# Layer norm in a two-block transformer: sums from a constant matrix as weights, mean, variance and root in all partitions, no broadcasts

## The chip, the cores and the metric

The kernel runs on one core of one Trainium2 chip. The metric is device time in microseconds of one execution, as the median of several runs. TensorE (PE) multiplies matrices, VectorE (DVE) and ScalarE (ACT) work elementwise, GpSimd (POOL) does elementwise work too, and SyncE (SP) issues most DMAs. Each engine takes its instructions from a queue of its own, in order, and waits on semaphores where it needs another engine's result.

## The reference

Two transformer blocks with two layers each run over 256 tokens of width 1024, the second with 16 tokens put in front (272). Between the matrix products stand ten layer norms of the residual stream. What the change touches is this:

```python
def layer_norm(x, g, b):
    xf = x.astype(jnp.float32)
    mu = jnp.mean(xf, -1, keepdims=True)
    var = jnp.mean(jnp.square(xf - mu), -1, keepdims=True)
    return ((xf - mu) * lax.rsqrt(var + EPS) * g + b).astype(x.dtype)
...
for i in range(DEPTH):
    ...
    x = layer_norm(DN_ALPHA * x + m, ln1_g[i], ln1_b[i])
    x = layer_norm(DN_ALPHA * x + conv_ffn(x, ffn_w_up[i], ffn_conv_w[i], ffn_conv_b[i], ffn_w_down[i]),
                   ln2_g[i], ln2_b[i])
    gate = jax.nn.sigmoid(x @ ple_w_gate[i] + ple_b_gate[i])
    x = x + gate * (p[i] @ ple_w_proj[i])
...
h = layer_norm_2(DEEPNORM_ALPHA * h + 0.5 * swiglu(h, ffn1_wg[l], ffn1_wu[l], ffn1_wd[l]),
               ln_gain[l, 0], ln_bias[l, 0])
...
h = layer_norm_2(DEEPNORM_ALPHA * h + mix, ln_gain[l, 1], ln_bias[l, 1])
h = layer_norm_2(DEEPNORM_ALPHA * h + 0.5 * swiglu(h, ffn2_wg[l], ffn2_wu[l], ffn2_wd[l]),
               ln_gain[l, 2], ln_bias[l, 2])
```

## The kernel before, in words

**Layout.** The residual X lies transposed in SBUF: 128 partitions, 8 chunks of the width, 256 or 272 tokens along the free axis. So a layer norm sums over partitions and chunks, and its mean and root differ from column to column. Each product of fp32 matrices is made of three matmuls of high and low halves (L405 to L407; L465, L466 and L468 are the same three in another order): XH and XL are the halves of X, wh and wl those of a weight chunk. The class Stream brings the weights in order: a DMA fills wraw, ScalarE makes wh (L315), VectorE wl (L317), some chunks ahead of their use.

**The norms.** Ten objects of the class LN follow one another, called LN1 to LN9 and the final norm here. LN1 to LN4 and LN8, LN9 have 256 tokens, LN5 to LN7 have 272 and so three token tiles instead of two. LN1 to LN4 stand ahead of the first block's up and gate projections and take the entry "early" of LN_AT. LN8 stands ahead of the query projection of the second block. While the product that makes X runs, evac (L566) adds each pair of chunks into X and gathers two partial sums, ln_d of X and ln_q of its squares, and raw_split makes XH and XL of the not yet normalised X.

**Hiding a norm.** The next product begins on that raw X: its first group runs over four output blocks and eight chunks kc. hook (L618) is called ahead of each kc and places the norm's steps there by the table LN_AT: stats, root and spread with the first finals. stats (L638) sums ln_d and ln_q over the partitions with one-column matmuls into a small tile [128 tokens, 2 to 4], and VectorE makes mean and variance of it. root takes the square root (ScalarE, L522) and one step of refinement (VectorE, L526 to L529, with a reciprocal). bcast (L535) turns a column of a small tile into a row in all partitions, by a transpose on TensorE: for the mean in root, for the root in spread. ScalarE copies both rows to SBUF (ln_m, ln_s). POOL waits for the root (L668) and subtracts the mean from X, two chunks at a time (L670). finals (L679) multiplies chunk by chunk with the root, which is read from PSUM (ln_w, L689), applies gain and bias (ScalarE L695 and L697, VectorE or POOL L699) and makes the new XL (L683). fix (L713) corrects the first group, which ran on raw X, in its output (L721).

**Order.** The program is written in the order of the calls, and each engine's queue follows it. W.fill(1) in hook issues a wh on ScalarE and the wl of the chunk before on VectorE at the kc's of LN_FILL. The final norm has no product to hide under: finish (L726) calls its steps one after the other, and the output's DMAs go out as chunks are done.

Of the kernel before, what the change touches and what calls it, by code (L numbers as in the profile page):

```python
# [10 lines left out]
F32 = mybir.dt.float32  # L11
F32R = mybir.dt.float32r
I32 = mybir.dt.int32
AF = mybir.ActivationFunctionType
ALU = mybir.AluOpType

P = 128
DM = 1024
# [6 lines left out]
EPS = 1e-5  # L25
# [2 lines left out]

AT = 96
XW, XO = 320, 12
HO = 4
XS = {"block1": 0, "block2": NMETA, "kv": 0}
# [113 lines left out]
TAIL = {"": 10, "gate0": 18, "gate1": 21, "aq": 24, "wo": 0, "cout": 14, "ao": 14}  # L148
LOOK = {"": 1, "aq": 2}

LN_AT = {"": (1, 2, 4), "early": (0, 1, 3)}
LN_FILL = {"": (0, 5), "aq": (0,), "f21": (0, 3)}

FILL = {"": (1, 2), "gate0": (0, 1), "gate1": (0, 1), "aq": (0, 1), "up1": (1, 1)}
# [69 lines left out]
def block_kernel(ctx: ExitStack, tc: tile.TileContext, wd, xin, pin, pos, vecs, con1, con2, wa2, fb, out):  # L224
# [3 lines left out]
    mm = nc.tensor.matmul  # L228
    V, A, G = nc.vector, nc.scalar, nc.gpsimd
# [133 lines left out]
    def cst(name, n, rows=P):  # L363
        return con[:rows, CON[name]:CON[name] + n]
# [25 lines left out]
    def aux():  # L390
        i = ps["n"][1] % 4
        if ps["mode"] == "aux":
            ps["n"][1] += 1
            if i >= 2:
                return ps["ext"].tile([P, 512], F32, tag="aux", name="aux")
        return ps["aux"].tile([P, 512], F32, tag="aux", name="aux")
# [111 lines left out]
    def token_tiles(T):  # L508
        return [0, P] + ([T - P] if T > 2 * P else [])
# [22 lines left out]
    def bcast(dst, r, T):  # L532

        for j, c0 in enumerate(token_tiles(T)):
            trp(dst[:, c0:c0 + P], r[:, j:j + 1].broadcast_to([P, P]), eye)  # L535
# [6 lines left out]
    class LN:  # L542
# [23 lines left out]
        def evac(self, m, n, psum):  # L566
            T = self.T
            xv = self.x(m, n)
            if m == 0:
                V.scalar_tensor_tensor(xv, xv, ALPHA, psum, op0=MUL, op1=ADD)  # L570
                self.s = self.buf("ln_s")[:, 0, :]
                V.tensor_tensor(self.s, self.x1(0), self.x1(1), op=ADD)
                if not self.final:
                    for k, nm in enumerate((self.g, self.b)):
                        c = VEC[nm] + self.j
                        split(self.XH[:, :, TT + k], self.XL[:, :, TT + k], vec[:, c:c + 8])
                return
            V.tensor_tensor(xv, psum, xv, op=ADD)  # L578
            sq = self.buf("ln_w", 2, 3)[:, :n, :]
            A.activation(sq, xv, AF.Square)  # L580
            if m <= 4:
                if m == 2:
                    self.D, self.Q = self.buf("ln_d", 2), self.buf("ln_q", 2)
                d, q = (self.x(0, 2), self.sq0) if m == 2 else (self.D, self.Q)
                V.tensor_tensor(self.D, d, xv, op=ADD)
                G.tensor_tensor(self.Q, q, sq, op=ADD)  # L586
                if m == 4:
                    D, Q = self.D, self.Q
                    self.D, self.Q = D[:, 0, :], Q[:, 0, :]
                    V.tensor_tensor(self.D, self.D, D[:, 1, :], op=ADD)  # L590
                    G.tensor_tensor(self.Q, self.Q, Q[:, 1, :], op=ADD)
            elif m == 6 or not self.final:
                V.tensor_tensor(self.D, self.D, xv[:, 0, :], op=ADD)
                V.tensor_tensor(self.Q, self.Q, sq[:, 0, :], op=ADD)
                self.parts = ((self.D, self.Q),)
            else:
                self.parts = ((self.D, self.Q), (xv[:, 0, :], sq[:, 0, :]))
            for i in range(m, m + n):
                self.raw_split(i)
# [18 lines left out]
        def hook(self, kc, name):  # L618

            h = LN_AT["early" if self.early else ""]  # L620
            if kc == h[0]:
                self.stats()
            if kc == h[1]:
                self.root()
            if kc == h[2]:
                self.spread()
                self.late = []
                self.finals(range(kc))
            elif kc > h[2]:
                self.finals((kc - 1,))  # L630
            if kc in LN_FILL.get(name, LN_FILL[""]):
                W.fill(1)
            if kc == 7:
                self.ndr = self.dls[:, 0, :]
                V.scalar_tensor_tensor(self.ndr, self.ndr, -1.0, self.R[:, :self.T], op0=MUL, op1=MUL)
                self.adds = []

        def stats(self):  # L638
            tt = token_tiles(self.T)
            n = len(tt)  # L640
            st = aux()
            order = [(i, w, j) for i in range(len(self.parts)) for w in range(2) for j in range(n)]
            for i, w, j in order:
                mm(st[:, 4 * w + j:4 * w + j + 1], self.parts[i][w][:, tt[j]:tt[j] + P], ones, start=(i, w, j) == order[0], stop=(i, w, j) == order[-1])  # L644
            self.dl = small.tile([P, 4], F32, tag="ln_dl", name="ln_dl")[:, :n]
            nd = small.tile([P, 4], F32, tag="ln_nd", name="ln_nd")[:, :n]
            self.v = small.tile([P, 4], F32, tag="ln_v", name="ln_v")[:, :n]
            V.tensor_scalar(self.dl, st[:, 0:n], 1.0 / DM, None, op0=MUL)
            V.scalar_tensor_tensor(nd, self.dl, -1.0, self.dl, op0=MUL, op1=MUL)
            V.scalar_tensor_tensor(self.v, st[:, 4:4 + n], 1.0 / DM, nd, op0=MUL, op1=ADD)  # L650

        def root(self):
            T = self.T
            DL = aux()
            bcast(DL, self.dl, T)
            self.dls = self.buf("ln_m")

            def between():
                A.activation(self.dls[:, 0, :], DL[:, :T], AF.Copy)

            self.r = rsqrt_eps(self.v, len(token_tiles(T)), between)
            if self.final:
                V.tensor_tensor(self.x(0, 2), self.x(0, 2), DL[:, None, :T].broadcast_to([P, 2, T]), op=SUB)
            if self.func:
                A.activation(dummy, epst, self.func)

            after = small.tile([P, 4], F32, tag="ln_nd", name="ln_nd")[:, :len(token_tiles(T))]
            G.tensor_copy(after, self.r)  # L668
            for m in range(2 if self.final else 0, 8, 2):
                G.tensor_tensor(self.x(m, 2), self.x(m, 2), self.dls.broadcast_to([P, 2, T]), op=SUB)  # L670

        def spread(self):
            self.R = aux()
            bcast(self.R, self.r, self.T)
            if not self.final:
                self.rs = self.buf("ln_s")
                A.activation(self.rs[:, 0, :], self.R[:, :self.T], AF.Copy)  # L677

        def finals(self, ms):  # L679
            T = self.T  # L680
# [4 lines left out]
            for m in ms:  # L685
                if m % 2 == 0:
                    self.t = self.buf("ln_w", 2, 3)
                t = self.t[:, m % 2, :]
                V.tensor_tensor(t, self.x1(m), self.R[:, :T], op=MUL)  # L689
                g, b = vc(self.g, self.j + m), vc(self.b, self.j + m)  # L690
                if self.final and m % 2:
                    A.activation(self.x1(m), t, AF.Identity, scale=g, bias=b)
# [33 lines left out]
        def finish(self):  # L726
            self.stats()
            self.root()
            self.spread()
            self.finals(range(8))  # L730


# [854 lines left out]
```

## Time and profile before

| | us |
|---|---|
| median of 3 runs (lowest, highest) | 1754.02 (1750.91, 1759.49) |
| the profiled execution | 1752.61 |
| its span on the core | 1750.8 |
| mean granted clock of TensorE | 0.986 of full speed |

The rows further down come from this one profiled execution. A matmul's record covers its passage through the array, so successive matmuls overlap: the pace is read from their starts, not from their durations. On the other engines too an instruction may begin shortly before its predecessor's end. A bracket at the end of a timeline row gives the idle time of that engine ahead of the instruction, and what ended it.

### The profile page before, as it was taken

The page shows a single profiled execution, that of the slowest core. Times are in us where ns is not written, and L with a number is a line of the kernel's source. Part 1 is how long each engine was busy: PE and PEld are TensorE (multiplying, and loading weights), DVE is VectorE, ACT ScalarE, POOL GpSimd, SP SyncE. Part 2 cuts the span into 40 slices and gives each one's busy share as a digit, 9 for nine tenths or more (in the row PEclk, how much of TensorE's full clock was granted, in tenths as well). Part 3 has the DMA queues.
Part 4 walks back from the last instruction along what each step waited for, and adds up shares of the span by engine and source line. Part 5 has one row for each costly group of instructions (what it writes and reads, how often), then busy time and mean ns, then how long its engine had stood idle before and what let it go on. Part 6 is the DMA issues. An engine that isn't in the chain of part 4 may idle for free. (4 is left out here: it accounts for less than half of the span.)

```text
span 1750.8 us, 34305 instructions
## 1 busy us (share of the span) xinstructions
PE 1710.1 (98%) x13954; PEld 1676.0 (96%) x13954; DVE 1212.7 (69%) x1951; ACT 997.3 (57%) x1575; POOL 217.8 (12%) x244
## 2 busy tenths in 40 slices
PE   7999999999999999999999999999999999999997
PEld 6999999997899999999999999999999999899997
DVE  6777898777579977755567787547665566787553
ACT  5666776566468765654445556445645553766542
POOL 6100211030012210200002030000200002020002
PEclk9999999999999999999999999999999999999998
DMA  6444466535445665365544627554446654237551
GB/s 224 133 140 161 134 217 211 199 122 201 146 144 161 219 208 185 122 230 178 181 157 135 226 98 240 171 180 170 154 162 196 196 181 162 71 135 253 193 181 37
DMA packets 82990, 298.18 MB, mean 170 GB/s; under 512 B 9319, under 2 KB 10487, under 8 KB 82832
## 3 DMA queue, kind: packets, MB, share of 16 engines
q1 hardware_dynamic: 82176, 294.13, 50.6%
q8 instruction: 109, 1.79, 0.4%
q0 software_dynamic: 656, 1.87, 0.4%
q14 instruction: 49, 0.40, 0.1%
HBM read 294.91 MB, written 1.05 MB: 169 GB/s over the span
## 5 line engine op out<-in xcount | busy, mean ns | idle before, releaser
L315 ACT ACTIVATE wh<-wraw 128x1024 fp32r<-128x1024 f32 (+1 forms) x557 | 578.8, 1055 | 352.8 <-PE acc L406 297.6
L405 PE MATMUL acc<-XH,wh 128*128 128x256 f32 (+3 forms) x2660 | 748.7, 281 | 2.8 <-ACT wh L315 1.7
L407 PE MATMUL acc<-XH,wl 128*128 128x256 f32 (+3 forms) x2660 | 745.5, 280 | 1.0 <-DVE wl L317 1.0
L406 PE MATMUL acc<-XL,wh 128*128 128x256 f32 (+3 forms) x2660 | 745.2, 280 | 0.0
L317 DVE TENSOR_TENSOR wl<-wraw,wh 128x1024 fp32r<-128x1024 f32 (+1 forms) x557 | 678.8, 1249 | 71.1 <-ACT wh L315 67.2
L405 PEld LDWEIGHTS acc<-XH,wh 128*128 128x128 f32 x2660 | 501.3, 188 | 3.7 <-ACT wh L315 1.9
L407 PEld LDWEIGHTS acc<-XH,wl 128*128 128x128 f32 x2660 | 500.7, 188 | 1.5 <-DVE wl L317 1.3
L406 PEld LDWEIGHTS acc<-XL,wh 128*128 128x128 f32 x2660 | 501.1, 188 | 0.0
L405 PE MATMUL acc<-hs,wh 128*128 128x256 f32 (+1 forms) x1044 | 291.8, 279 | 0.0
L406 PE MATMUL acc<-hs,wh 128*128 128x256 f32 (+1 forms) x1044 | 290.6, 278 | 0.0
L407 PE MATMUL acc<-hs,wl 128*128 128x256 f32 (+1 forms) x1044 | 290.6, 278 | 0.0
L406 PEld LDWEIGHTS acc<-hs,wh 128*128 128x128 f32 x1044 | 195.9, 188 | 0.2
L405 PEld LDWEIGHTS acc<-hs,wh 128*128 128x128 f32 x1044 | 195.9, 188 | 0.2
L407 PEld LDWEIGHTS acc<-hs,wl 128*128 128x128 f32 x1044 | 195.9, 188 | 0.0
L1312 DVE SCALAR_TENSOR_TENSOR sg<-acc,sg 128x272 f32<-128x272 f32 (+1 forms) x84 | 36.2, 432 | 185.5 <-ACT sg L1311 185.4
L586 POOL TENSOR_TENSOR ln_q<-ln_w 128x512 f32<-128x512 f32 (+1 forms) x10 | 14.2, 1422 | 978.2 <-ACT ln_w L580 978.2
L580 ACT ACTIVATE ln_w<-X 128x512 f32<-128x512 f32 (+3 forms) x40 | 21.3, 533 | 92.2 <-DVE X L578 92.1
L1120 POOL TENSOR_TENSOR gl<-cv,gl 128x256 f32<-128x256 f32 x44 | 39.2, 892 | 185.6 <-ACT gl L1119 102.1
L578 DVE TENSOR_TENSOR X<-acc,X 128x512 f32<-128x512 f32 (+3 forms) x40 | 22.4, 561 | 56.0 <-PE acc L407 56.0
L1311 ACT ACTIVATE sg<-acc 128x272 f32<-128x272 f32 (+1 forms) x84 | 32.5, 389 | 48.0 <-PE acc L407 47.5
L689 DVE TENSOR_TENSOR ln_w<-X,aux 128x256 f32<-128x256 f32 (+1 forms) x80 | 33.1, 417 | 37.3 <-ACT ln_s L677 29.3
L695 ACT ACTIVATE XH<-ln_w,vec 128x256 fp32r<-128x256 f32 (+1 forms) x72 | 42.3, 600 | 27.0 <-DVE ln_w L689 26.3
(418 smaller groups left out, 2311.8 us busy)
## 6 DMA issues: line engine op xcount, KB each, us to landing
wraw<-wd SPq DMA_DIRECT2D x555, 512.0 KB, 4.2
X<-xin SPq DMA_DIRECT2D x4, 272.0 KB, 6.1
out_t<-X SPq DMA_DIRECT2D x3, 256.0 KB, 2.7
wraw<-wd SPq DMA_DIRECT2D x2, 256.0 KB, 4.2
praw<-pin POOLq DMA_DIRECT2D x2, 256.0 KB, 2.9
fpt<-con POOLq DMA_DIRECT2D x2, 256.0 KB, 4.1
cum<-con POOLq DMA_DIRECT2D x1, 408.0 KB, 4.3
vec<-vecs SPq DMA_DIRECT2D x1, 283.0 KB, 7.0
```

The costliest lines, as they stand in the source:

```text
L315: A.activation(h[:, k], r[:, k], AF.Copy)
L317: self.low = lambda h=h, l=l, r=r, i=i: [V.tensor_tensor(l[:, k], r[:, k], f32(h[:, k]), op=SUB) for k in self.cuts(i)]
L405: mm(o, wh, xh, start=start, stop=False)
L406: mm(o, wh, xl, start=False, stop=False)
L407: mm(o, wl, xh, start=False, stop=stop)
L578: V.tensor_tensor(xv, psum, xv, op=ADD)
L580: A.activation(sq, xv, AF.Square)
L689: V.tensor_tensor(t, self.x1(m), self.R[:, :T], op=MUL)
L695: A.activation(self.XH[:, m, self.t0:TT], t, AF.Identity, scale=g, bias=b)
L1120: G.tensor_tensor(gl, t[:, 0, :], gl, op=MUL)
L1311: A.activation(s, psum[:, 0, :], AF.Silu)
L1312: V.scalar_tensor_tensor(s, psum[:, 1, :], 0.5, s, op0=MUL, op1=MUL)
```

## The change

The sums are made by two matmuls for each pair of partial sums, with a 128 x 128 matrix of 1/256 (the constant c256, which mid in L605 uses already) as weights: each partition then holds the sum of every token. Mean, variance and root are worked out there on all tokens, with tiles [128, 256] or [128, 272]. The broadcasts, spread, and the small tile ln_dl are gone. The subtraction of the mean from the first two chunks moves from POOL to VectorE. ln_w takes the root from the SBUF tile ln_s instead of PSUM. LN_AT calls root right behind stats. AT keeps later addresses where they were.

```diff
-AT = 96
+AT = 224
...
-LN_AT = {"": (1, 2, 4), "early": (0, 1, 3)}
+LN_AT = {"": (1, 1, 4), "early": (0, 0, 3)}
...
-                    self.D, self.Q = D[:, 0, :], Q[:, 0, :]
+                    self.D, self.Q, self.scratch = D[:, 0, :], Q[:, 0, :], Q
...
             if kc == h[2]:
-                self.spread()
                 self.late = []
                 self.finals(range(kc))
...
-                V.scalar_tensor_tensor(self.ndr, self.ndr, -1.0, self.R[:, :self.T], op0=MUL, op1=MUL)
+                V.scalar_tensor_tensor(self.ndr, self.ndr, -1.0, self.rs[:, 0, :], op0=MUL, op1=MUL)
...
         def stats(self):
-            tt = token_tiles(self.T)
-            n = len(tt)
-            st = aux()
-            order = [(i, w, j) for i in range(len(self.parts)) for w in range(2) for j in range(n)]
-            for i, w, j in order:
-                mm(st[:, 4 * w + j:4 * w + j + 1], self.parts[i][w][:, tt[j]:tt[j] + P], ones, start=(i, w, j) == order[0], stop=(i, w, j) == order[-1])
...
+            self.S = [aux()[:, :self.T] for _ in range(2)]
+            n = len(self.parts)
+            for w in range(2):
+                for i, p in enumerate(self.parts):
+                    mm(self.S[w], cst("c256", P), p[w], start=i == 0, stop=i == n - 1)
 
         def root(self):
             T = self.T
-            DL = aux()
-            bcast(DL, self.dl, T)
+            sd, sq = self.S
             self.dls = self.buf("ln_m")
...
-            self.r = rsqrt_eps(self.v, len(token_tiles(T)), between)
-            if self.final:
-                V.tensor_tensor(self.x(0, 2), self.x(0, 2), DL[:, None, :T].broadcast_to([P, 2, T]), op=SUB)
+            dl, v, t = self.dls[:, 0, :], self.scratch[:, 0, :], self.scratch[:, 1, :]
+            self.rs = self.buf("ln_s")
+            r = self.rs[:, 0, :]
+            A.activation(dl, sd, AF.Copy, scale=0.25)
+            V.scalar_tensor_tensor(v, dl, -1.0, dl, op0=MUL, op1=MUL)
+            V.scalar_tensor_tensor(v, sq, 0.25, v, op0=MUL, op1=ADD)
+            A.activation(r, v, AF.Sqrt, bias=epst)
+            V.tensor_scalar(v, v, EPS, None, op0=ADD)
+            V.tensor_tensor(self.x(0, 2), self.x(0, 2), self.dls.broadcast_to([P, 2, T]), op=SUB)
+            V.reciprocal(r, r)
+            V.tensor_tensor(t, r, r, op=MUL)
+            V.scalar_tensor_tensor(t, t, -0.5, v, op0=MUL, op1=MUL)
+            V.scalar_tensor_tensor(r, t, 1.5, r, op0=ADD, op1=MUL)
             if self.func:
                 A.activation(dummy, epst, self.func)
 
-            after = small.tile([P, 4], F32, tag="ln_nd", name="ln_nd")[:, :len(token_tiles(T))]
-            G.tensor_copy(after, self.r)
-            for m in range(2 if self.final else 0, 8, 2):
+            after = small.tile([P, 4], F32, tag="ln_nd", name="ln_nd")
+            G.tensor_copy(after, r[:, :4])
+            for m in (2, 4, 6):
                 G.tensor_tensor(self.x(m, 2), self.x(m, 2), self.dls.broadcast_to([P, 2, T]), op=SUB)
-
-        def spread(self):
-            self.R = aux()
-            bcast(self.R, self.r, self.T)
-            if not self.final:
-                self.rs = self.buf("ln_s")
-                A.activation(self.rs[:, 0, :], self.R[:, :self.T], AF.Copy)
...
-                V.tensor_tensor(t, self.x1(m), self.R[:, :T], op=MUL)
+                V.tensor_tensor(t, self.x1(m), self.rs[:, 0, :], op=MUL)
```

In what follows, names stand for tiles and "128x256" for partitions and elements. VectorE's queue at LN1 before, from the sums to the second multiplication with the root (aux is the PSUM tile with the sums, later that with the broadcast root):

```order
L648 TENSOR_SCALAR ln_dl<-aux 128x2
L649 SCALAR_TENSOR_TENSOR ln_nd<-ln_dl 128x2
L650 SCALAR_TENSOR_TENSOR ln_v<-aux,ln_nd 128x2
L317 TENSOR_TENSOR wl<-wraw,wh 128x1024
L523 TENSOR_SCALAR ln_v<-ln_v 128x2
L526 RECIPROCAL rs_r<-rs_r 128x2
L527 TENSOR_TENSOR rs_t<-rs_r 128x2
L528 SCALAR_TENSOR_TENSOR rs_t<-rs_t,ln_v 128x2
L529 SCALAR_TENSOR_TENSOR rs_r<-rs_t,rs_r 128x2
L689 TENSOR_TENSOR ln_w<-X,aux 128x256
L699 TENSOR_SCALAR X<-ln_w,vec 128x256
```

The same stretch of VectorE's queue after (with the line numbers of the changed file):

```order
L653 SCALAR_TENSOR_TENSOR ln_q<-ln_m 128x256
L654 SCALAR_TENSOR_TENSOR ln_q<-aux,ln_q 128x256
L656 TENSOR_SCALAR ln_q<-ln_q 128x256
L657 TENSOR_TENSOR X<-X,ln_m 128x2x256
L658 RECIPROCAL ln_s<-ln_s 128x256
L659 TENSOR_TENSOR ln_q<-ln_s 128x256
L660 SCALAR_TENSOR_TENSOR ln_q<-ln_q 128x256
L661 SCALAR_TENSOR_TENSOR ln_s<-ln_q,ln_s 128x256
L317 TENSOR_TENSOR wl<-wraw,wh 128x1024
L680 TENSOR_TENSOR ln_w<-X,ln_s 128x256
L690 TENSOR_SCALAR X<-ln_w,vec 128x256
```

The weight split wl stood between variance and root and now stands behind the root; a subtraction on X has come in, and ln_w reads ln_s.

ScalarE's queue at the same place, before:

```order
L315 ACTIVATE wh<-wraw 128x1024
L522 ACTIVATE rs_r<-ln_v,epst 128x2
L659 ACTIVATE ln_m<-aux 128x256
L665 ACT_TABLE_LOAD
L665 ACTIVATE dummy<-epst 128x1
L677 ACTIVATE ln_s<-aux 128x256
```

And after:

```order
L652 ACTIVATE ln_m<-aux 128x256
L655 ACTIVATE ln_s<-ln_q,epst 128x256
L663 ACT_TABLE_LOAD
L663 ACTIVATE dummy<-epst 128x1
L315 ACTIVATE wh<-wraw 128x1024
```

The wh of the weight stream stood ahead of the square root and now stands behind it and the table load; the copy of the broadcast root is gone.

## Rows read from the trace of the kernel before

**Rows 1.** the page's busy shares: engine, busy us (share) xinstructions.

```profile
PE 1710.1 (98%) x13954; PEld 1676.0 (96%) x13954; DVE 1212.7 (69%) x1951; ACT 997.3 (57%) x1575; POOL 217.8 (12%) x244
```

**Rows 2.** TensorE's waits: line <- releaser: us in total, times, longest.

```profile
PE aux L406 <- DVE XL L683: 3.8, 1, 3.8
...
PE acc L465 <- ACT sg L1139: 2.7, 1, 2.7
...
PE acc L412 <- DVE XL L506: 2.4, 1, 2.4
...
PE acc L405 <- DVE cv L1115: 0.9, 1, 0.9
...
PE acc L405 <- DVE ln_d L721: 0.2, 1, 0.2
```

**Rows 3.** timeline of TensorE, LN1: start, us, instruction [idle before <-releaser].

```profile
185.64 0.28 PE L407 MATMUL acc<-ph,wl 128*128 128x256 f32 x1
...
186.76 0.28 PE L466 MATMUL acc<-XH,wl 128*128 128x258 f32 x1
...
191.01 0.28 PE L407 MATMUL acc<-XH,wl 128*128 128x258 f32 x1
...
191.47 0.28 PE L406 MATMUL acc<-XL,wh 128*128 128x258 f32 x1
```

**Rows 4.** timeline of TensorE around one sum of L605.

```profile
155.27 0.28 PE L407 MATMUL acc<-O,wl 128*128 128x256 f32 x1
...
155.94 0.28 PE L406 MATMUL acc<-O,wh 128*128 128x256 f32 x1
```

**Rows 5.** timeline of VectorE, LN1; the last line is LN3.

```profile
187.20 1.22 DVE L317 TENSOR_TENSOR wl<-wraw,wh 128x1024 fp32r<-128x1024 f32 x1
...
188.99 0.17 DVE L529 SCALAR_TENSOR_TENSOR rs_r<-rs_t,rs_r 128x2 f32<-128x2 f32 x1
192.03 0.42 DVE L689 TENSOR_TENSOR ln_w<-X,aux 128x256 f32<-128x256 f32 x1 [2.87 <-ACT ln_s L677]
192.49 0.82 DVE L699 TENSOR_SCALAR X<-ln_w,vec 128x256 f32<-128x256 f32 x1
...
525.40 0.42 DVE L689 TENSOR_TENSOR ln_w<-X,aux 128x256 f32<-128x256 f32 x1 [4.74 <-ACT ln_s L677]
```

**Rows 6.** timeline of ScalarE and POOL, LN1.

```profile
191.54 0.38 ACT L677 ACTIVATE ln_s<-aux 128x256 f32<-128x256 f32 x1 [1.16 <-PE aux L535]
...
189.36 5.11 POOL L670 TENSOR_TENSOR X<-X,ln_m 128x512 f32<-128x512 f32 x4
```

**Rows 7.** VectorE by shape: xcount | busy us, mean ns | idle before, releasers.

```profile
L526 DVE RECIPROCAL rs_r<-rs_r 128x2 f32<-128x2 f32 x9 | 1.4, 158 | 0.0
...
L526 DVE RECIPROCAL rs_r<-rs_r 128x4 f32<-128x4 f32 x2 | 0.3, 171 | 0.0
...
L699 DVE TENSOR_SCALAR X<-ln_w,vec 128x256 f32<-128x256 f32 x13 | 12.4, 957 | 0.5
...
L689 DVE TENSOR_TENSOR ln_w<-X,aux 128x272 f32<-128x272 f32 x24 | 10.3, 430 | 12.0 <-ACT ln_s L677 12.0
```

**Rows 8.** all instructions of line 564: ns min/median/max, first and last start.

```profile
L564 DVE SCALAR_TENSOR_TENSOR XL<-X,vec,XH x72: 472/496/1608, 158.9 to 1553.9; 128x256 fp32r<-128x256 f32 x48, 128x272 fp32r<-128x272 f32 x24
```

**Rows 9.** timeline of VectorE, LN8; TensorE's window behind it: us, busy (x), PEclk, DMA.

```profile
1484.07 0.42 DVE L689 TENSOR_TENSOR ln_w<-X,aux 128x256 f32<-128x256 f32 x1 [7.15 <-POOL X L670]
1484.52 3.35 DVE L699 TENSOR_SCALAR X<-ln_w,vec 128x256 f32<-128x256 f32 x1
...
1489.30:1494.80 5.50, 5.43 (x25) 0.50 0.01 1
```

**Rows 10.** timeline of VectorE and POOL, final norm.

```profile
1741.09 0.16 DVE L529 SCALAR_TENSOR_TENSOR rs_r<-rs_t,rs_r 128x2 f32<-128x2 f32 x1
1741.17 0.68 DVE L663 TENSOR_TENSOR X<-X,aux 128x512 f32<-128x512 f32 x1
...
1741.45 3.86 POOL L670 TENSOR_TENSOR X<-X,ln_m 128x512 f32<-128x512 f32 x3
```

More of the change, by code (lines that the diff above doesn't have):

```diff
@@ L645, in stats @@
[L645 to L650, printed above, removed]
+            self.S = [aux()[:, :self.T] for _ in range(2)]
@@ L652, in root @@
+            n = len(self.parts)
+            for w in range(2):
+                for i, p in enumerate(self.parts):
+                    mm(self.S[w], cst("c256", P), p[w], start=i == 0, stop=i == n - 1)
         def root(self):
             T = self.T
-            DL = aux()
-            bcast(DL, self.dl, T)
+            sd, sq = self.S
             self.dls = self.buf("ln_m")
-            def between():
-                A.activation(self.dls[:, 0, :], DL[:, :T], AF.Copy)
-            self.r = rsqrt_eps(self.v, len(token_tiles(T)), between)
@@ L728, in finish @@
             self.root()
-            self.spread()
             self.finals(range(8))
```

## The prediction, made before the changed kernel ran

> **What bounds the kernel now.** I read the page's busy shares first. TensorE is busy for 1710.1 of 1750.8 us [rows 1], so the time falls only by what is taken off TensorE's queue, and it rises wherever TensorE is made to wait. Next I read the view of TensorE's waits [rows 2], which tells at which layer norms TensorE already waits for the VectorE work behind them: 3.8 us for XL of L683 (the norm ahead of the query projection, LN8), 2.7 us for sg, where ScalarE itself waits for the new X (LN4), 2.4 us for XL of L506 (LN2), 0.9 us for cv (LN1) and 0.2 us for the corrected group of L721 (LN7). At such a norm a VectorE that comes later by d makes TensorE later by d, and a TensorE that comes earlier only waits longer. Last I read the timelines around one norm [rows 3 to 6], which give the price of each step.
>
> **What TensorE saves.** Before, four one-column matmuls lie between the start of the L407 matmul at 185.64 and the L466 at 186.76: 1.12 us for what is otherwise two steps of TensorE's pace, 0.115 us here (the mean of [rows 1], 1710.1 us over 13954 matmuls, is 0.12), so 0.89 us for the sums [rows 3]. The broadcast of the root lies between 191.01 and 191.47: 0.46 us for two steps of 0.115, so 0.23 us, and there are two broadcasts. A 256-token norm now costs 0.89 + 0.46 = 1.35 us of TensorE. The new sums are two matmuls of the shape that L605 already runs; one of those lies between 155.27 and 155.94 and costs 0.67 - 0.23 = 0.44 us [rows 4], so two cost 0.88 us. The saving is 0.47 us a norm, for six norms (a tenth, the final one, has nothing beside it). The three 272-token norms have a third token tile, so half as many sums and broadcasts again: 2.02 us against 0.94, a saving of 1.08. Together 6 x 0.47 + 3 x 1.08 = 6.1 us, if TensorE has no one to wait for.
>
> **What VectorE pays.** Before, its chain from sum to root works on 2 to 4 columns, under 0.2 us a step: it gives way to a weight split of 1.22 us and ends at 188.99 + 0.17 = 189.16. Then VectorE idles 2.87 us until the root has been broadcast and copied, and L689 starts at 192.03 [rows 5]. After, the same steps are 256 columns wide. From the rows: a two-input step of this width starts the next 0.45 us on (0.42 at 192.03), a ScalarE pass 0.38 us [rows 6], a 512-wide subtraction 0.68 us [rows 10].
>
> The reciprocal has no wide instance in this trace. By width it takes 158 ns at 2 columns and 171 ns at 4 [rows 7], 6.5 ns a column, so about 0.158 + 254 x 0.0065 = 1.8 us at 256. As a low bound I take it as cheap as any other step, 0.42 us; as a high one 9 ns a column, 2.4 us, since two such rows fix a slope poorly. I take 1.8, because the slope comes from the instruction itself. The Trainium skill, page "VectorE: DVE Perf Modes", section "First, the fixed hardware budget", says that the reciprocal is an iterative divide with a repeat count of 8; at the 0.96 GHz of that page's specifications that makes an estimate of 2.1 us, and a sum about 2 us higher than mine (seven places, 0.3 us each). The two rows of widths agree with it in kind.
>
> LN1, step by step. TensorE has the mean's sum by about 186.3; ScalarE's copy makes it 186.8; the square 187.25, the variance 187.7, the root on ScalarE 188.2, + eps 188.6, the subtraction on X (moved here from POOL) 189.3, the reciprocal 191.1, three more steps 192.4. The order puts the weight split, which stood inside the old chain, behind the new one: 1.15 us more. L689 then starts at about 193.5 instead of 192.03: **+1.5 us**, at LN1, LN2 and LN4, which have the same order and the same 2.9 us of idle time. In the rows by shape L689 waits 12.0 us for ln_s at three 272-token norms [rows 7], 4.0 us each and 1.1 us more than LN1; there the shift is 1.5 - 1.1, less a little because nothing is queued ahead of ScalarE's pass: +0.3 us. LN3 waits 4.74 us at this place [rows 5], 1.9 us more than LN1, and takes all of it: 0. On ScalarE the wh pass of the weight stream, which stood ahead of the old root, now waits behind the new one until 188.2 and the table load, more than 1.5 us later; the stream is prepared chunks ahead of TensorE, so I cost that at nothing, and were that cover gone TensorE would wait those 1.5 us for wh.
>
> **What POOL's subtractions cost.** POOL starts its subtractions when the root is ready; before, four take 5.11 us from 189.36 [rows 6]. L689 reads PSUM there and is not held up (0.42 at 192.03, while POOL works), but the scale and bias of L699, which reads and writes SBUF, is: 0.82 us at 192.49 [rows 5], 957 ns in the mean of 13 [rows 7], some 0.54 us more than L689 of the same width. L564, with two inputs in SBUF, has a median of 496 ns and a maximum of 1608 [rows 8]. At LN8 one L699 waits through all that POOL has queued, 3.35 us [rows 9]. After, ln_w takes the root from SBUF, so it has two inputs in SBUF, as L564 has, and it starts just after the root, together with POOL's three remaining subtractions. So L689 loses its immunity. Bounds: 0 (it slips in between), and 2.8 us a norm (three subtractions, 3.86 us by [rows 10], waited through in full, less 2 x 0.54 us that the two L699 wait already). I take 0.8 us for each of the first two ln_w, between the 0.54 that L699 waits in the mean and the 1.1 of L564's worst: **+1.6 us a norm** at LN1 to LN7. This is the largest term and the least sure. The Trainium skill, page "GPSIMD Engine Reference", section "1. Specifications", says that POOL shares its SBUF interfaces with VectorE and that instructions with two SBUF inputs contend; L564's and L699's rows agree, and no row here shows ln_w in that form.
>
> **LN8** goes the other way. L689 waits 7.15 us there for POOL's first subtraction [rows 9], since POOL has loads of its own queued ahead; VectorE now does this one itself, so L689 starts about 3 us sooner. The L699 behind it still meets POOL's queue. Of the 3.8 us for which TensorE waits I take back 2.0. The bounds are 0 and 6.4: behind the wait the granted clock is 0.50 over 5.50 us, TensorE's 1.2 GHz level, with 25 matmuls in 5.43 us [rows 9] that take 25 x 0.115 = 2.9 us at 2.4 GHz, so 2.6 us go with the wait if it goes whole.
>
> **LN9** keeps its TensorE saving of 0.5 us; I see no wait behind it and let its slack carry the rest.
>
> **The final norm** has nothing to hide it. Before, the root is ready at 1741.09 + 0.16 = 1741.25 and POOL's subtractions start at 1741.45 [rows 10]. The sums end about 0.6 us sooner, then the chain as in LN1: copy 0.4, square and variance 0.9, root and + eps 0.8, subtraction 0.7, reciprocal 1.8, three steps 1.35, so a root at about 1744.8 and POOL's subtractions 3.5 us later; 0.2 more for ln_w beside them: **+3.7 us** (+2.1 if the reciprocal is cheap).
>
> **The sum.** 3 x 1.5 + 3 x 0.3 + 7 x 1.6 - 2.0 - 0.5 + 3.7 = 4.5 + 0.9 + 11.2 + 1.2 = +17.8 us. TensorE's saving at LN1 to LN8 is not in it: TensorE waits there anyway. The profiled execution took 1752.61 us, 1.4 us under the median of the runs, so +17.8 is 1770.4 from the one and 1771.8 from the other; I say **1771 us**.
>
> **The rivals.** (a) POOL does not hold ln_w up. For it speaks that L689 is not held up today, against it that L564 is. At 0 instead of 1.6 us a norm the sum is 17.8 - 11.2 = +6.6, **about 1760 us**; the point that decides is 0.3 us a norm, above which the change is slower by more than can be told from none. (b) The wide reciprocal costs what any step costs, and (a) holds too. It takes 1.4 us off each of LN1, LN2, LN4 and the tail (-5.6), and TensorE's saving comes through at LN3 and LN5 to LN7 (0.5 + 3 x 1.1 = 3.7): 6.6 - 9.3 = -2.7, **about 1751 us**. For it speaks that VectorE is busy for a far smaller share than TensorE, against it the slope of [rows 7]. (c) POOL keeps VectorE off through all that it has queued, as at LN8: 2.8 instead of 1.6 us at seven norms (+8.4), and with it a reciprocal of 2.4 us at LN1, LN2, LN4 to LN7 and the tail (+4.2): 17.8 + 12.6, **about 1784 us**. TensorE's waits at LN2 and LN4, 2.4 and 2.7 us now, would then pass the 3.8 us behind which the clock stood at 0.50 at LN8, which could cost 2.6 us more at each, so 1789 at the far end. (d) Faster in earnest: VectorE's lateness is nowhere waited for, so that the whole 6.1 us come through, LN8 gives back all of its 6.4, and only the tail's 2.1 us (with a cheap reciprocal) are paid: -10.4, **about 1743 us**. The waits of [rows 2] at LN1, LN2 and LN4 speak against it.
>
> **How the numbers follow.** About 0.5% (8.8 us) is what a measurement of this kernel can tell from no change. My forecast's case has a chance of 0.52 and (c) 0.14; both are slower by more than that: 0.66. (a) has 0.15 and (b) 0.09, both within it: 0.24. (d) has 0.10 and is faster. The range leaves out (d) and the far end of (c), and begins just under (b): 1749 to 1787.
>
> **What would show it.** The profile after should show the wide reciprocal at 1.6 to 2.4 us (0.4 would fell the chain's term); L689 at LN1 starting near 193.5, not 192.0; ln_w of more than 0.8 us where POOL's subtractions run (0.42 throughout would fell the largest term); TensorE's waits for cv, XL and sg longer by 2 to 3 us a norm; LN8's wait shorter, with less time at a granted clock of 0.50 behind it; the time from the last stream matmul to the end longer by 3.5 us. Wrong altogether it is if TensorE's waits stay as they are: then the slack was there, and the time is near (a).

## The result, and the profile after

| | us |
|---|---|
| before, median of 5 runs | 1754.8 |
| changed, median of 5 runs (lowest, highest) | 1782.44 (1778.61, 1787.38) |
| ratio, 95% interval | 1.0165 (1.0144 to 1.0186) |
| changed, the profiled execution (its span) | 1779.6 (1777.5) |

The change makes the kernel 27.6 us slower. The prediction said 1771 us, slower, with a range of 1749 to 1787; the time lies inside it, on the far side of the forecast.

The page's first section of the changed kernel: engine, busy us (share) xinstructions.

```profile
PE 1709.6 (96%) x13852; PEld 1667.7 (94%) x13852; DVE 1270.2 (71%) x1950; ACT 996.2 (56%) x1566; POOL 226.3 (13%) x235
```

Against [rows 1] TensorE does 102 matmuls fewer and its share falls from 98 to 96%: it waits more. VectorE is busy for 57.5 us more. For whom TensorE waits is in the view of its waits, which answers to [rows 2] (line <- releaser: us in total, times, longest):

```profile
PE acc L406 <- DVE XL L674: 14.4, 27, 1.9
...
PE acc L405 <- DVE ln_d L712: 5.8, 6, 1.0
PE acc L407 <- DVE wl L317: 4.5, 4, 2.4
...
PE acc L405 <- DVE cv L1105: 3.3, 2, 1.7
...
PE aux L406 <- DVE XL L674: 2.1, 1, 2.1
...
PE acc L412 <- DVE XL L506: 0.2, 1, 0.2
```

The first line is new: 27 waits for the new XL (L674 is the L683 of before), on chunk after chunk of the product behind a norm. The waits for L712 (before: L721) grew from 0.2 to 5.8 us, for cv from 0.9 to 3.3. LN8's wait, the row with aux, fell from 3.8 to 2.1. The 2.4 us for L506, at LN2, are nearly gone, since TensorE now waits earlier in that stretch, 2.4 us for wl and 1.5 for XL. The waits for wl, the low half of a weight chunk, which VectorE makes, grew to 4.5 us (2.4 at LN2, 0.7 at LN3, 1.4 at LN4) from this in the kernel before:

```profile
PE acc L407 <- DVE wl L317: 1.0, 2, 0.5
```

VectorE at LN1 (start, us, instruction [idle before <-releaser]), which answers to [rows 5], and POOL beside it:

```profile
186.50 0.42 DVE L653 SCALAR_TENSOR_TENSOR ln_q<-ln_m 128x256 f32<-128x256 f32 x1 [1.87 <-ACT ln_m L652]
...
188.03 0.29 DVE L656 TENSOR_SCALAR ln_q<-ln_q 128x256 f32<-128x256 f32 x1 [0.64 <-ACT ln_s L655]
188.24 0.68 DVE L657 TENSOR_TENSOR X<-X,ln_m 128x512 f32<-128x512 f32 x1
188.84 1.75 DVE L658 RECIPROCAL ln_s<-ln_s 128x256 f32<-128x256 f32 x1
...
191.88 1.22 DVE L317 TENSOR_TENSOR wl<-wraw,wh 128x1024 fp32r<-128x1024 f32 x1
193.02 0.42 DVE L680 TENSOR_TENSOR ln_w<-X,ln_s 128x256 f32<-128x256 f32 x1
193.47 1.26 DVE L690 TENSOR_SCALAR X<-ln_w,vec 128x256 f32<-128x256 f32 x1
194.66 1.50 DVE L680 TENSOR_TENSOR ln_w<-X,ln_s 128x256 f32<-128x256 f32 x1
196.20 1.27 DVE L690 TENSOR_SCALAR X<-ln_w,vec 128x256 f32<-128x256 f32 x1
197.39 0.41 DVE L680 TENSOR_TENSOR ln_w<-X,ln_s 128x256 f32<-128x256 f32 x1
```

```profile
192.03 1.12 POOL L666 COPY ln_nd<-ln_s 128x4 f32<-128x4 f32 x1 [16.13 <-DVE ln_s L661]
193.12 4.20 POOL L668 TENSOR_TENSOR X<-X,ln_m 128x512 f32<-128x512 f32 x3
```

The reciprocal takes 1.75 us. The first ln_w starts at 193.02 and is free of POOL, the second takes 1.50 us in the middle of POOL's 4.20, and each scale and bias 1.27 instead of the 0.82 of [rows 5]. POOL suffers too: its copy of four columns takes 1.12 us beside the weight split, and 0.44 at the final norm.

The stretches of TensorE's timeline from one norm's sums to the next show where the time went. The sums of LN1 to LN9 and of the final norm start at 185.75, 371.48, 516.51, 705.88, 931.74, 1032.07, 1230.73, 1473.88, 1554.95 and 1737.64 before, and at 185.37, 375.08, 523.90, 714.80, 945.63, 1049.21, 1251.90, 1496.64, 1574.64 and 1758.95 after; the spans end at 1750.8 and 1777.5.

| stretch behind | LN1 | LN2 | LN3 | LN4 | LN5 | LN6 | LN7 | LN8 | LN9 | final |
|---|---|---|---|---|---|---|---|---|---|---|
| predicted, us | +3.1 | +3.1 | +1.6 | +3.1 | +1.9 | +1.9 | +1.9 | -2.0 | -0.5 | +3.7 |
| measured, us | +4.0 | +3.8 | +1.5 | +5.0 | +3.2 | +4.0 | +1.6 | -3.1 | +1.6 | +5.4 |

Each kernel was profiled in one execution, and executions of the changed kernel lie up to 9 us apart as a whole, so single columns are read with care; the sum is 27.1, and LN1 starts 0.4 us sooner, which makes the 26.7 us between the spans.

### The profile page after: what moved, and what is told of

It reads as the page before. It is cut to its first block, busy times and chain, and to the rows that moved or that the text cites. A ratio compares the mean times of both kernels' runs of the same rounds, so it can differ in the third digit from the quotient of the medians.

```text
span 1777.5 us, 34116 instructions
## 1 busy us (share of the span) xinstructions
PE 1709.6 (96%) x13852; PEld 1667.7 (94%) x13852; DVE 1270.2 (71%) x1950; ACT 996.2 (56%) x1566; POOL 226.3 (13%) x235
## 4 chain that ended last, share of the span: by engine, by line
PE 57%; DVE 8%; POOL 2%; issue 1%; ACT 1%; POOLq 0%; DVEq 0%; ACTq 0%
PE acc L405 18%; PE acc L407 18%; PE acc L406 18%; POOL X L690 2%; DVE wl L317 2%; DVE ln_w L680 1%; DVE X L690 1%; DVE ln_s L658 1%; DVE XL L564 1%; DVE XL L674 0%; DVE X L578 0%; DVE ln_d L712 0%; DVE X L657 0%; PE aux L1465 0%; ACT ln_s L655 0%
## 5 line engine op out<-in xcount | busy, mean ns | idle before, releaser
L315 ACT ACTIVATE wh<-wraw 128x1024 fp32r<-128x1024 f32 (+1 forms) x557 | 579.1, 1055 | 352.3 <-PE acc L406 297.7
L406 PE MATMUL acc<-XL,wh 128*128 128x256 f32 (+3 forms) x2660 | 749.6, 282 | 14.4 <-DVE XL L674 14.4
L406 PEld LDWEIGHTS acc<-XL,wh 128*128 128x128 f32 x2660 | 501.2, 188 | 20.7 <-DVE XL L674 20.2
L406 PE MATMUL acc<-hs,wh 128*128 128x256 f32 (+1 forms) x1044 | 291.7, 279 | 0.0
L406 PEld LDWEIGHTS acc<-hs,wh 128*128 128x128 f32 x1044 | 195.9, 188 | 0.2
L1102 ACT ACTIVATE cv<-acc,vec 128x256 f32<-128x256 f32 x80 | 40.7, 558 | 29.9 <-PE acc L407 29.7
```

Source lines behind the costliest of these rows:

```text
L315: A.activation(h[:, k], r[:, k], AF.Copy)
L406: mm(o, wh, xl, start=False, stop=False)
L1102: A.activation(t[:, e, :], psum[:, e, :], AF.Identity, scale=cw(2, e, j), bias=vc("cb", i * 44 + e * 22 + j))
```

## The experiments

Changes to the time are given as ratios to the kernel before, which ran beside each on the same chip. "Against the changed kernel" is the difference of two ratios times 1754.8 us, good to 4 to 7 us (the two intervals taken together).

### The root in PSUM, the reciprocal left out, and both

The first run, e1, moves ln_w's second input back to PSUM. POOL's small copy, which holds its subtractions back until the root is there, then waits for the last step but one of the chain (t) instead of the last (r):

```diff
-            V.scalar_tensor_tensor(r, t, 1.5, r, op0=ADD, op1=MUL)
+            self.R = aux()[:, :T]
+            V.scalar_tensor_tensor(self.R, t, 1.5, r, op0=ADD, op1=MUL)
...
-            G.tensor_copy(after, r[:, :4])
+            G.tensor_copy(after, t[:, :4])
...
                 self.late = []
+                A.activation(self.rs[:, 0, :], self.R, AF.Copy)
                 self.finals(range(kc))
...
-                V.tensor_tensor(t, self.x1(m), self.rs[:, 0, :], op=MUL)
+                V.tensor_tensor(t, self.x1(m), self.R, op=MUL)
```

> The changed kernel, but the last step of the root writes to PSUM and ln_w reads the root there, as before the change; ScalarE copies it to ln_s. Theory (two terms: the wide chain makes VectorE late, and ln_w with two SBUF inputs waits for POOL): the second ln_w falls from 1.50 to about 0.42 us at LN1, some 1 us less a norm, about 1774 us. Rival (whatever VectorE does next that shares the port waits through POOL's subtractions, so the source of ln_w only moves the wait to the scale and bias): no gain, 1780 to 1784 us.

1764.12 us, ratio 1.0063 (1.0040 to 1.0086): 17.9 us less than the changed kernel, about twice what the theory gave it. VectorE of this run, by line and shape (xcount | busy us, mean ns | idle before), and TensorE's waits for XL:

```profile
L682 DVE TENSOR_TENSOR ln_w<-X,aux 128x256 f32<-128x256 f32 x56 | 22.6, 410 | 1.1 <-POOL X L670 0.6 <-ACT ln_s L627 0.5
L692 DVE TENSOR_SCALAR X<-ln_w,vec 128x256 f32<-128x256 f32 x13 | 14.1, 1086 | 0.5
```

```profile
PE acc L406 <- DVE XL L676: 3.1, 7, 0.8
```

ln_w takes 410 ns in the mean (559 in the changed kernel), the scale and bias 1086 (1437), and TensorE's 27 waits of 14.4 us for XL become 7 of 3.1. The rival, that the wait moves to the scale and bias, falls, though at LN1 a first XL of 1.18 us instead of 0.41 takes over a part of it.

The 17.9 us are not all ln_w's source. At LN1 POOL's subtractions begin 1.04 us ahead of the first ln_w here (192.86 and 193.90), in the changed kernel 0.10 us behind it. At the final norm they begin 5.53 us behind the chain's first step on VectorE (1754.01 - 1748.48) instead of 6.00 (1766.91 - 1760.91). What this earlier start is worth was not tried by itself; e6 below changes the source alone.

The second run, e2, takes out the reciprocal. A scaling stands in its place and in that of "+ eps", so that the root is a constant:

```diff
-            V.tensor_scalar(v, v, EPS, None, op0=ADD)
+            V.tensor_scalar(v, v, 0.0, 1.0, op0=MUL, op1=ADD)
...
-            V.reciprocal(r, r)
+            V.tensor_scalar(r, r, 0.0, 0.05, op0=MUL, op1=ADD)
```

> The changed kernel with a scaling in the place of the wide reciprocal (the root is then a constant, so the normalisation is left out). Theory: the step falls from 1.75 to about 0.3 us, and as VectorE is waited for behind LN1 to LN8 and at the end, 1.45 us come back at about 8 of the 10 norms: about 1770 us. Rival (the waits come from POOL's port and the chain's length is hidden): only the final norm gains, about 1781 us.

1771.01 us, 1.0096 (1.0064 to 1.0128): 12.1 us less than the changed kernel, as the theory had it, and TensorE's waits for XL fall from 14.4 to 3.4 us. The reciprocal is on TensorE's path at most of the norms and not only at the last.

The run e7 has both edits.

> Both at once in the changed kernel: the root in PSUM and a scaling in the place of the reciprocal (the root is a constant, the normalisation is left out). Theory (two causes that add up, 18 us for the source and 11 us for the reciprocal): all of the 27.6 us come back, 1752 to 1755 us. Rival (they cover each other, as both delay the same XL): 1758 to 1763 us.

1752.76 us, 0.9987 (0.9975 to 0.9999). Against the changed kernel that is 31 us, and the two alone gave 17.9 + 12.1 = 30: they add up and do not cover each other. With these two causes gone the rest of the change, with TensorE's saving, LN8's gain and the other wide steps, comes out within 0.25% of the kernel before. TensorE's waits for wl are still 3.7 us in e7, so neither cause makes these alone.

### ln_w's source alone, in the kernel before

e6 makes the converse test: the kernel before, with the one input of ln_w changed.

```diff
-                V.tensor_tensor(t, self.x1(m), self.R[:, :T], op=MUL)
+                V.tensor_tensor(t, self.x1(m), self.R[:, :T] if self.final else self.rs[:, 0, :], op=MUL)
```

> The kernel before, in which ln_w alone takes the root from ln_s in SBUF, at the nine norms that have it (the final norm reads PSUM as it did). Theory (ln_w's source is the larger part of what the change costs): 1.0 to 1.5 us a norm, about +12 us, 1766 us. Rival (the source matters only where the root comes late, as in the changed kernel): within 3 us of before.

1766.91 us, 1.0069 (1.0050 to 1.0088): +12.1 us from the place of one operand. The theory is met; that the source would matter only behind a late root is not. VectorE at LN1 of this run, the first two steps and the last XL:

```profile
191.40 1.40 DVE L689 TENSOR_TENSOR ln_w<-X,ln_s 128x256 f32<-128x256 f32 x1 [2.87 <-ACT ln_s L677]
192.84 1.27 DVE L699 TENSOR_SCALAR X<-ln_w,vec 128x256 f32<-128x256 f32 x1
...
202.12 0.42 DVE L683 TENSOR_TENSOR XL<-X,XH 128x256 fp32r<-128x256 f32 x1 [0.38 <-POOL X L699]
```

The sums of this run start at 185.12. The third ln_w begins 9.69 us behind them (8.79 before), the last XL 17.00 (15.09): of the 1.9 us, 0.9 arise at the first two chunks and 1.0 behind them.

### Which of POOL's work ln_w meets

e3 let POOL subtract as soon as the mean is there, by leaving out its copy of the root.

```diff
-            after = small.tile([P, 4], F32, tag="ln_nd", name="ln_nd")
-            G.tensor_copy(after, r[:, :4])
```

> The changed kernel without POOL's copy of the root, so that POOL subtracts the mean as soon as it is there, beside the chain to the root. Theory: ln_w and the scale and bias are free of POOL (2.8 us less a norm), the chain's two-input steps wait for it instead (1 to 2 us more), and the subtractions leave the final norm's path (about 4 us): 1765 to 1772 us. Rival (the port costs the same wherever POOL runs): 1778 to 1782 us, the final norm's share alone.

1785.22 us, 1.0182 (1.0152 to 1.0212), no less than the changed kernel. But this edit also drops a small tile, and matmuls became slower, mostly in the first block; the last experiment below takes that up. e5 keeps the tile and copies the mean instead:

```diff
-            G.tensor_copy(after, r[:, :4])
+            G.tensor_copy(after, dl[:, :4])
```

> The changed kernel with POOL's copy taking the mean instead of the root, so that POOL subtracts as soon as the mean is there; the small tile stays, so no address moves. Theory (POOL's scale and bias holds ln_w up through all eight chunks, and the subtractions are only half of it): TensorE's waits shrink by about 5 us, 1774 to 1778 us. Rival (the subtractions are all of the port's cost): the 1.3 us a norm and the end's 2 us of the run with the root in PSUM come back here too, about 1765 us.

1769.15 us, 1.0092 (1.0074 to 1.0111): 12.8 us less than the changed kernel, between the two expectations, and too near both to choose. VectorE at LN1 of this run:

```profile
189.51 1.78 DVE L657 TENSOR_TENSOR X<-X,ln_m 128x512 f32<-128x512 f32 x1
191.22 1.74 DVE L658 RECIPROCAL ln_s<-ln_s 128x256 f32<-128x256 f32 x1
...
195.39 0.42 DVE L680 TENSOR_TENSOR ln_w<-X,ln_s 128x256 f32<-128x256 f32 x1
195.84 0.41 DVE L690 TENSOR_SCALAR X<-ln_w,vec 128x256 f32<-128x256 f32 x1
196.17 0.42 DVE L680 TENSOR_TENSOR ln_w<-X,ln_s 128x256 f32<-128x256 f32 x1
```

VectorE's own subtraction now waits for POOL, 1.78 instead of 0.68 us; the reciprocal, with one input, runs beside POOL at its usual 1.74 us; ln_w and the scale and bias are free. At LN1 the collision is paid once, not three times. At LN8, where POOL has loads of its own queued ahead, its subtractions start late all the same, and the first ln_w waits through all three of them:

```profile
1495.40 4.38 DVE L680 TENSOR_TENSOR ln_w<-X,ln_s 128x256 f32<-128x256 f32 x1
```

What is left of the gap between e5 and e1 I sought in chunks 4 to 7, where POOL does the scale and bias. e8 gave those to ScalarE, as chunks 2 and 3 have it.

```diff
-                    if m in (2, 3) and not self.final:
+                    if m > 1 and not self.final:
```

> The changed kernel with the scale and bias of chunks 4 to 7 on ScalarE, as chunks 2 and 3 have it, so POOL has the subtractions alone. Theory (POOL's scale and bias waits for the port behind VectorE's ln_w, and XL waits for it): TensorE's waits for XL of L674, 14.4 us now, fall by more than half, 1770 to 1775 us. Rival (ScalarE, with two passes a chunk, becomes as late as POOL was, or the XL waits come from the subtractions alone): 1780 to 1786 us.

1785.47 us, 1.0180 (1.0164 to 1.0196): the rival's range. The lines of this run show why it decides nothing:

```profile
L674 DVE TENSOR_TENSOR XL<-X,XH 128x256 fp32r<-128x256 f32 x48 | 20.1, 419 | 8.7 <-ACT X L688 8.7
L674 DVE TENSOR_TENSOR XL<-X,XH 128x272 fp32r<-128x272 f32 x24 | 10.4, 435 | 4.1 <-ACT X L688 4.1
```

ScalarE, with two passes a chunk, keeps XL waiting for 12.8 us. So e12 went the other way: the kernel before, with ln_w from SBUF in chunks 4 to 7 alone.

```diff
-                V.tensor_tensor(t, self.x1(m), self.R[:, :T], op=MUL)
+                V.tensor_tensor(t, self.x1(m), self.R[:, :T] if self.final or m < 4 else self.rs[:, 0, :], op=MUL)
```

> The kernel before, in which ln_w takes the root from ln_s in SBUF for chunks 4 to 7 alone, when POOL's subtractions are over and POOL does scale and bias (the first four chunks read PSUM as before). Theory (POOL's scale and bias and VectorE's ln_w hold each other up there, the part of the cost that my prediction left out): the last XL of a norm comes 0.8 us later at 256 tokens and 1.2 us at 272, six of the nine waited for, +5 to +8 us, about 1761 us. Rival (only the stretch with POOL's subtractions costs time): within 2 us of before.

1760.74 us, 1.0022 (1.0006 to 1.0037): +3.9 us (+1.1 to +6.5 by the interval). That is above no change and a little under the theory's range, and the time alone does not exclude the rival's 2 us; the trace speaks for the theory. POOL's scale and bias by shape, first of the kernel before, then of this run:

```profile
L699 POOL TENSOR_SCALAR X<-ln_w,vec 128x256 f32<-128x256 f32 x27 | 23.8, 881 | 15.7 <-DVE ln_w L689 15.2
L699 POOL TENSOR_SCALAR X<-ln_w,vec 128x272 f32<-128x272 f32 x12 | 12.7, 1055 | 9.6 <-DVE ln_w L689 9.5
```

```profile
L699 POOL TENSOR_SCALAR X<-ln_w,vec 128x256 f32<-128x256 f32 x27 | 30.0, 1122 | 13.9 <-DVE ln_w L689 13.9
L699 POOL TENSOR_SCALAR X<-ln_w,vec 128x272 f32<-128x272 f32 x12 | 16.8, 1413 | 8.4 <-DVE ln_w L689 8.4
```

POOL's scale and bias grows from 881 to 1122 ns and from 1055 to 1413, while ln_w itself stays short (414 ns): here POOL is the one held up, and the last XL waits for it. At LN1 the last XL begins 200.84 - 185.75 = 15.09 us behind the start of the sums before, and 200.34 - 184.60 = 15.74 here. In the changed kernel it is 204.46 - 185.37 = 19.09.

e10 joined the two mends, the root in PSUM and POOL's copy of the mean. Its edit against e1:

```diff
-            G.tensor_copy(after, t[:, :4])
+            G.tensor_copy(after, dl[:, :4])
```

> The changed kernel with both mends of the port: the root in PSUM for ln_w, and POOL subtracting as soon as the mean is there. Theory (VectorE's scale and bias still waits for POOL in the run e1, VectorE's subtraction waits in the run e5): the last XL of LN1 comes 0.7 us earlier than in e1, 1757 to 1761 us. Rival (the wait only moves into the chain to the root): 1763 to 1766 us, as e1.

1762.71 us, 1.0054 (1.0038 to 1.0070), which can't be told from e1's 1.0063. VectorE's subtraction of X waits for POOL here as in e5 (1.78 us at LN1). The last XL of LN1 does come 0.7 us earlier, as the theory had it, 16.65 us behind the sums (203.16 - 186.51) against 17.34 in e1 (203.59 - 186.25); how much of that reaches TensorE is too little for this measurement. Against e5 e10 is 6.7 us shorter (good to 4). Between those two only the place of the root differs, with ScalarE's copy of it to ln_s, and POOL's subtractions are out of the way at LN1 in both: from the third ln_w to the last XL it takes 7.08 us in e5 and 6.31 in e10 (6.30 in the kernel before, 7.07 in the changed one). So ln_w from SBUF costs 0.8 us there by what it does to POOL's scale and bias.

### What the change has that is good: the subtraction on VectorE

e4 takes it into the kernel before, for four chunks instead of two, out of PSUM:

```diff
-            if self.final:
-                V.tensor_tensor(self.x(0, 2), self.x(0, 2), DL[:, None, :T].broadcast_to([P, 2, T]), op=SUB)
+            for m in (0,) if self.final else (0, 2):
+                V.tensor_tensor(self.x(m, 2), self.x(m, 2), DL[:, None, :T].broadcast_to([P, 2, T]), op=SUB)
...
-            for m in range(2 if self.final else 0, 8, 2):
+            for m in range(2 if self.final else 4, 8, 2):
```

> The kernel before, but VectorE subtracts the mean from the first four chunks (the first two at the final norm, as it was) out of PSUM, and POOL only from the others. Theory: VectorE is idle there for 2.9 us or more, POOL is through before the scale and bias come, and LN8 no longer waits for POOL: 5 to 10 us less than before, about 1746 us. Rival (VectorE's 1.3 us come on top of its chain): 0 to 8 us more than before.

1745.81 us, 0.9952 (0.9937 to 0.9968): 8.4 us less than before and faster than both kernels. VectorE at LN1 of this run:

```profile
188.02 1.28 DVE L663 TENSOR_TENSOR X<-X,aux 128x512 f32<-128x512 f32 x2
190.90 0.42 DVE L689 TENSOR_TENSOR ln_w<-X,aux 128x256 f32<-128x256 f32 x1 [1.61 <-ACT ln_s L677]
191.36 0.42 DVE L699 TENSOR_SCALAR X<-ln_w,vec 128x256 f32<-128x256 f32 x1
```

The two subtractions fill 1.28 of the 2.87 us that VectorE idled in [rows 5], POOL is through with its two before ln_w comes, and the scale and bias falls to 0.42 us.

e9 also starts the root's broadcast and the first multiplications one step sooner (its edit against e4):

```diff
-LN_AT = {"": (1, 2, 4), "early": (0, 1, 3)}
+LN_AT = {"": (1, 2, 3), "early": (0, 1, 2)}
```

> The kernel before with the first two subtractions on VectorE (as in the run e4) and, with X ready sooner, the root's broadcast and the first multiplications one step earlier in the next product (LN_AT 1, 2, 3 and 0, 1, 2). Theory (the end of VectorE's work on a norm is what TensorE waits for at LN1 to LN8): about 1 us less than e4 at each of seven norms, 1738 to 1742 us. Rival (the root is not ready one step earlier, and TensorE waits at the broadcast instead): 1746 to 1752 us.

1745.35 us, 0.9946 (0.9924 to 0.9967): no different from e4. The last XL at LN1 of this run:

```profile
199.14 0.43 DVE L683 TENSOR_TENSOR XL<-X,XH 128x256 fp32r<-128x256 f32 x1 [0.75 <-ACT XH L695]
```

Reckoned from the sums, the first ln_w comes 1.3 us sooner than in e4 (4.93 instead of 6.21), but the last XL only 0.4 (13.67 instead of 14.08), since it now waits for ScalarE's XH. Neither expectation was right: TensorE's wait at the broadcast didn't grow, and nothing that could be measured came back.

### The gap AT

e11 undoes one line of the change, which the prediction passed over:

```diff
-AT = 224
+AT = 96
```

> The changed kernel with AT = 96, so that the tiles behind the gap lie 128 bytes lower than in the kernel before. In the run e3, which dropped a small tile and so moved addresses, matmuls stepped 115.1 ns apart instead of 113.6. Theory (the addresses set TensorE's pace, and AT = 224 is in the change to keep them): the same slower pace, 1795 to 1805 us. Rival (e3's pace came from elsewhere): 1780 to 1785 us.

1793.18 us, 1.0225 (1.0195 to 1.0255): 10.5 us more than the changed kernel, the theory's direction with a smaller size. TensorE from 260 to 340 us, a stretch without a wait in either (window: us, busy (x instructions), PEclk, DMA share, GB/s), first the changed kernel, then this one:

```profile
260.00:340.00 80.00, 80.00 (x706) 1.00 0.65 209
```

```profile
260.00:340.00 80.00, 80.00 (x699) 1.00 0.65 214
```

At the same granted clock it gets through 699 matmuls instead of 706, 1.0% fewer; e3 had 698. From 800 to 900 us the two counts are 814 and 812, so the first block bears most of it. Not all matmuls are slower: the records of L406 that read hs last 281 ns in the median instead of 275, those that read XL 275 in both. With e11's share taken off, e3 would stand at 1.012, near e5's 1.0092; that the addresses are all of e3's loss is likely, but the errors are too large to show it.

## Why the prediction was right, and where it was not

**The reciprocal: right.** Its slope of 6.5 ns a column, read from rows of 2 and 4 columns, gave 1.8 us; it takes 1.75 (e2 shows that it is waited for: 12.1 us). The 2.1 us that I had estimated from the iterative divide of the Trainium skill ("VectorE: DVE Perf Modes", section "First, the fixed hardware budget") are 20% too high; the measurement decides.

**VectorE's lateness at LN1: right.** The first ln_w starts 7.65 us behind the sums instead of 6.28, +1.4 where I said +1.5, and the third, behind the two scale and bias steps, 12.02 instead of 8.79, +3.2 where the sum of my two terms was +3.1. At LN5 the first ln_w is not later at all (+0.3 in the prediction) and the third 2.0 us later (1.9).

**VectorE and POOL holding each other up (port contention): the right mechanism, the wrong size.** I put +11.2 us on it, 1.6 us at each of seven norms; e1 gives back 17.9, with the earlier start of POOL and the final norm in it. In the first chunks the sum was nearly right, though not its parts: I had two ln_w held up and the scale and bias no more than before, and in the trace the first ln_w runs free, the second waits 1.1 us, and the two scale and bias steps wait longer. What I left out is a second partner: POOL has work behind its subtractions, and ln_w from SBUF holds that up, too, in chunks 4 to 7 (e12: +3.9 us in the kernel before; e5 against e10 at LN1: 0.8 us). The final norm, which e1 mends as well, meets both. LN1's stretch grew by 4.0 us while its third ln_w came 3.2 us later; the 0.8 between them arose there. The step of the prediction that failed is "+1.6 us a norm", which looked at the first two chunks alone: by the lines of LN1 it is 1.8 us there (1.1 for the second ln_w, 0.8 for the two scale and bias steps, against their times before) and 0.8 behind them, some 2.6 together. The Trainium skill's sentence on the shared interfaces ("GPSIMD Engine Reference", section "1. Specifications") covers both partners: instructions with two SBUF inputs contend, and e6 shows 12.1 us from that alone; I had applied it to one of the two places. Of the two rows that I had agreeing with it, L564's bear on it and L699's do not, since L699 has one SBUF input.

**The weight stream: right for wh, wrong for wl.** "the stream is prepared chunks ahead of TensorE, so I cost that at nothing" was said of the wh pass on ScalarE, and TensorE's waits for wh are no longer than before (1.7 us instead of 2.9). But I put nothing either on a wait of TensorE for wl, which VectorE makes, and that grew from 1.0 to 4.5 us. A late VectorE delays the stream, too: in e6, where the order of the queues is that of before, the waits for wl are 4.8 us. What they add to the whole time was not tried by itself.

**LN9: wrong.** "I see no wait behind it and let its slack carry the rest" gave -0.5; it measured +1.6. TensorE waits 2.1 us for XL and 1.0 us for L712 behind LN9 now, and waited for nothing there before. A view of waits shows where slack is used up, not how much is left elsewhere.

**LN8: right in kind.** -3.1 us where I took -2.0. TensorE's wait falls from 3.8 to 2.1 us, and the stretch at a granted clock of 0.50 behind it from the 5.50 us of [rows 9] to 3.40 us (1510.80 to 1514.20 us of the changed kernel), as the prediction had it in kind. Its scale and bias still waits through POOL's queue, as this row of the changed kernel shows beside the 3.35 us of [rows 9]:

```profile
1504.19 4.24 DVE L690 TENSOR_SCALAR X<-ln_w,vec 128x256 f32<-128x256 f32 x1
```

**The final norm: too small.** +5.4 instead of +3.7. POOL in both kernels, first the changed one, then the one before (its subtractions are in [rows 10]):

```profile
1766.91 3.93 POOL L668 TENSOR_TENSOR X<-X,ln_m 128x512 f32<-128x512 f32 x3
1771.23 2.65 POOL L690 TENSOR_SCALAR X<-ln_w,vec 128x256 f32<-128x256 f32 x3 [0.39 <-DVE ln_w L680]
```

```profile
1745.30 1.63 POOL L699 TENSOR_SCALAR X<-ln_w,vec 128x256 f32<-128x256 f32 x3
```

From the start of the sums to POOL's subtractions it is 7.96 us instead of 3.81, 4.2 more where I had 3.5; and POOL's last steps take 1.0 us more, the same partner as in chunks 4 to 7. (By the terms of the prediction the cheap reciprocal leaves +2.3 here, 3.7 - 1.4; its +2.1 drops the 0.2 for ln_w as well.)

**TensorE's saving.** It is there (102 matmuls fewer, no broadcast) and swallowed, as forecast: with both costs taken out, e7 is no more than 0.25% faster than before. So rival (c), at 1784 us, came nearest in time, though not by its mechanism: POOL did not keep VectorE off through all that it had queued, except at LN8. My likeliest case was short by 10 us for the reasons above, and that the time still lies inside the range is owed to the width that (c) gave it, which is in part luck.

## What to carry to other kernels

Where VectorE and GpSimd work side by side, an operand's place can cost more than an operation's length: moving one input of a multiplication from PSUM to SBUF cost 12 us here without adding an instruction. When you price such a collision, list everything that the other engine has queued over the whole stretch, not only what starts at the same time. And where the bound engine waits for another's outcome, look for that engine's idle gaps first: here a subtraction moved into one (e4) brought 8.4 us, and 102 matmuls taken off the bound engine brought next to nothing.

## What the runs showed of the hardware that I had not expected

A shift of 128 bytes in where tiles lie in SBUF changed the pace of some of TensorE's matmuls: 699 matmuls in 80 us instead of 706 at a granted clock of 1.00 (e11; e3 likewise, 698), mostly in the first block. What in the addresses does this was not tried.

POOL's subtractions don't hold the wide reciprocal up: 1.74 us in e5, where POOL works beside most of it, against 1.75. That it has one input does not explain it by itself: the "+ eps" step has one input, too, and beside POOL's subtractions at the final norm of e5 it takes 1.33 us, in the changed kernel 0.29:

```profile
1752.59 1.33 DVE L656 TENSOR_SCALAR ln_q<-ln_q 128x256 f32<-128x256 f32 x1 [0.64 <-ACT ln_s L655]
```

Where a VectorE step with two SBUF inputs, or a scale and bias from SBUF to SBUF, met POOL, it was not always VectorE that lost: the second ln_w of the changed kernel takes 1.50 us instead of 0.42, but in e12 ln_w stays at 414 ns and POOL's scale and bias grows from 881 to 1122. What decides between the two was not tried.
